# Other temporaries for the embedding's product and the stored gates, the gates' columns ahead of the sums of x, some low parts on GpSimd, and spaced gate rows and scores

## The chip, the core and the metric

The kernel runs on one core of a Trainium2 chip. The core has five engines with queues of their own: PE (TensorE: matmuls, transposes; its weight loads are listed as PEld), DVE (VectorE), ACT (ScalarE), POOL (GpSimd) and SP (SyncE, which here only issues DMAs; POOL issues some as well). An engine runs its queue in order; semaphores make it wait for others. The metric is the device time of one execution in microseconds (us), lower is better. Times of one kernel vary a little, so several runs stand beside each other, and one further execution is recorded by the hardware profiler.

## The reference

One block of a hybrid decoder on 512 positions of width 1024, all in float32, one sequence:

```
hn   = rmsnorm(x, g_mix);  proj = hn @ w_in            # 1024 x 14344
xa, ba, ca, za, q, k, v, o, zb, ig, fg, ga, gb = split(proj)
ya   = (ba * causal_short_conv(ca * xa) * silu(za)) @ w_a_out
hb   = mlstm(q, k, v, ig + b, log_sigmoid(fg + b))     # 4 heads, dk 256, dv 512
yb   = (sigmoid(o) * rmsnorm(hb) * silu(zb)) @ w_b_out
x    = x + (sigmoid(ga) * ya + sigmoid(gb) * yb) @ w_o
gate = sigmoid(rmsnorm(x, g_ple) @ w_ple_gate)
out  = rmsnorm(x + gate * (p @ w_ple), g_final)
```

In the mLSTM each head weights its scores q.k by exponentials of running sums of the gates: cumulative sums of log_sigmoid(fg), a running maximum of ig minus these sums, and the normaliser max(|den|, exp(-m)). The kernel computes it over all 512 positions at once, as a causal attention in blocks of 128.

## The kernel before

**Products.** Matmuls take float32 operands as two parts, hi and lo. ACT copies a tile into hi (`whi` for weights, line 142), DVE subtracts it from the tile to give lo (`wlo`, line 143), and PE forms hi*hi + hi*lo + lo*hi (lines 191 to 193). Weights come in operands of 512 rows and 512 columns, `wraw`, loaded by SP (line 125) into four buffers, and are split in two halves; `wlo31` is the low part of operand 3, half 1. An operand is used by 48 matmuls.

**Strassen blocks.** Where two column blocks belong together (GB; V with O of a head; ZB of two heads; GA), `strassen` makes the output of 2 x 2 blocks from seven products instead of eight. The combinations of hn, `hs`, are made once (POOL makes the sums `hsf`, `left` splits them into hi and lo). The combinations of weights are made in the raw buffers by DMAs that POOL issues with accumulation (line 146), each after the split of the half that it overwrites. Product j is done in two halves i; after each, a small generator (t1 to t6) snapshots sums with ACT (tags `s`, `v`), forms an output `c` on DVE (line 300, three buffers) and hands it to a sink.

**Order.** The order of each engine's instructions is the order in which the program emits them. After each half of a product, `step` calls `tick`: first the generators handed over at the step before, then one half of the next weight split, then one step of every generator in `active`. So one `yield` in a generator moves the rest of it one step, 12 matmuls, later. `drain` runs what is still active without anything in between.

**Around the change.** In the start stage, p @ w_ple is kept in eight temporaries `ples`, which take buffers of the tags in a string, in the order in which SP stores them (line 506). Temporaries of tags e, s and v have two buffers, of c three. Operands 1 and 2 then give the four columns of the first convolution channel block (`xa`, `ca`, `ba`, `za`), whose tasks use temporaries of tags e and c. Next PE computes the gates `psg` (line 565) from `wg`, the hi and lo parts of the gate columns of w_in in one tile, filled on DVE (lines 557, 558). A Strassen block for GB follows (operands 3 to 9), with two generators beside it: `left` (the splits of hs) and `gate_rows`, which works on `rows`, 4 partitions of 512. It ends with PE's transposes `ptc` of the rows; the queries and keys of head 0 (operands 10 and 11) come next on PE.

Per head: Q and K (a block), `scores` beside the Strassen block of V and O, the weighted sums `pv`, and after heads 0 and 2 a Strassen block for ZB of two heads. Its sink `sink_z` finishes the even head's gate and stores that of the odd head, `z_d`, which is loaded into `gt` in the odd head. In `scores`, step k of seven makes the score block `sc` k on PE and its exponentials `e` on ACT; the product `pp` (DVE), its hi copy `pr` (ACT), its lo part (DVE) and the running sum (POOL) follow.

Of the kernel before, what the change touches and what calls it, by code (L numbers as in the profile page):

```python
# [36 lines left out]
def hybrid_block(ctx, tc, x, p, g_mix, w_in, conv_w, conv_b, w_a_out, b_gates, g_head,  # L37
# [347 lines left out]
    bg = sp.tile([NH, 2], F32, name="bg")  # L385
    ss = sp.tile([P, NT], F32, name="ss")
    tmp = [sp.tile([P, NT], F32, name=f"rtmp{i}") for i in range(3)]
    ples = [temp(u, f"ple{i}") for i, u in enumerate("ssvvccee")]
    xin = sp.tile([P, NT, D], F32, name="xin", tag="xin")
    hnf = sp.tile([P, KT, S], F32, name="hnf")  # L390
    sq = hnf[:, 0:2, :].rearrange("p k s -> p (k s)")
# [120 lines left out]
    for h in range(2):  # L512
        for m in range(4):
# [5 lines left out]
            elif m % 2:  # L519
                split_half(2, m // 2)  # L520

    a11, a12 = (hnf[:, c * HC:(c + 1) * HC, :H2] for c in range(2))
    a21, a22 = (hnf[:, c * HC:(c + 1) * HC, H2:] for c in range(2))
    hsf = [sp.tile([P, HC, H2], F32, name=f"hsf{i}", tag=f"hsf{i}", align_bytes=256) for i in range(2)]
# [23 lines left out]
    for m in range(4):  # L548
# [6 lines left out]
    for g in range(2):  # L555
        src = wg_raw[:, :, g * NH:(g + 1) * NH]
        dve.tensor_copy(wg[:, :, 32 * g:32 * g + NH], src)
        dve.tensor_tensor(wg[:, :, 64 + 32 * g:64 + 32 * g + NH], src,
                          wg[:, :, 32 * g:32 * g + NH].bitcast(F32), ALU.subtract)
    for r in (0, 32):  # L560
        dve.tensor_copy(sel[r:r + NH], ident[r:r + NH, r:r + NH].unsqueeze(2).broadcast_to([NH, NH, P]))

    psg = ps_x.tile([P, S], F32, name="psg", tag="x")
    for k in range(KT):
# [13 lines left out]
    def gate_rows():  # L578
        for g, dst in enumerate((li, lf)):
            act.activation(dst, psg[64 + 32 * g:64 + 32 * g + NH, :], AF.Identity, bias=bg[:, g:g + 1])  # L580
        yield
        for g, dst in enumerate((li, lf)):
            dve.tensor_tensor(dst, dst, psg[32 * g:32 * g + NH, :], ALU.add)
        yield

        act.activation(la, lf, AF.Abs)
        act.activation(la, la, AF.Exp, scale=-1.0)
        yield
        dve.tensor_scalar(u1, la, 1.0, None, ALU.add)
        dve.scalar_tensor_tensor(off, u1, 1.0, la, ALU.subtract, ALU.subtract)  # L590
        yield
        act.activation(la, u1, AF.Ln)
        yield
        dve.scalar_tensor_tensor(lf, lf, 0.0, off, ALU.min, ALU.add)
        dve.tensor_tensor(lf, lf, la, ALU.subtract)
        yield
# [24 lines left out]
        dve.tensor_copy(nmr[0:NH], negm)  # L621
        yield
        dve.tensor_tensor(nmr[32:32 + NH], negm, nmr[0:NH].bitcast(F32), ALU.subtract)
        dve.tensor_tensor(mrow, negm, bcf, ALU.subtract)
        yield

        ptc = ps_x.tile([P, S], F32, name="ptc", tag="x")
        for n in PAIR.values():
            pe.transpose(ptc[:, 4 * n:4 * n + 4], ul[:, n, :], ident[:NH, :NH])
        for t in range(NT):  # L630
            pe.transpose(ptc[:, 40 + 4 * t:44 + 4 * t], mrow[:, t * P:(t + 1) * P], ident[:NH, :NH])
        yield
        dve.tensor_copy(colsb, ptc[:, :56])
        act.activation(enm.rearrange("p t h -> p (t h)"), colsb[:, 40:], AF.Exp)
# [39 lines left out]
            for u in range(2):  # L674
                nc.gpsimd.dma_start(yt_d[h][u], yt[u].bitcast(F32))

    def scores(h, qk, pr, pp):

        pnb = ps_x.tile([P, S], F32, name="pnb", tag="x")
        pe.matmul(pnb, lhsT=sel[:, h, :], rhs=nmr, start=True, stop=True)  # L680
# [7 lines left out]
        for k in range(NT + 3):  # L688
            if k < NT:
# [6 lines left out]
                for t in range(k, NT):  # L696
                    c = 4 * PAIR[(k, t)] + h
                    src = negd[:, t, :] if t == k else negb[:, t * P:(t + 1) * P]
                    act.activation(e[k][:, t * P:(t + 1) * P], src, AF.Exp, bias=colsb[:, c:c + 1])
            if 0 <= k - 1 < NT:  # L700
                j = k - 1
                sl = slice(POFF[j], POFF[j] + S - T0[j])
                dve.scalar_tensor_tensor(pp[:, sl], sc[j][:, T0[j]:], DK ** -0.5, e[j][:, T0[j]:], ALU.mult, ALU.mult)
                act.activation(pr[0][:, sl], pp[:, sl], AF.Copy)
            if 0 <= k - 2 < NT:
                j = k - 2
                sl = slice(POFF[j], POFF[j] + S - T0[j])
                dve.tensor_tensor(pr[1][:, sl], pp[:, sl], pr[0][:, sl].bitcast(F32), ALU.subtract)
            if 1 <= k - 3 + 0 < NT:
                j = k - 3  # L710
                sl = slice(POFF[j], POFF[j] + S - T0[j])
                pool.tensor_tensor(pp[:, T0[j]:S], pp[:, T0[j]:S], pp[:, sl], ALU.add)
            yield

    def head(h):
        qk, vv = [], []
# [25 lines left out]
                act.activation(gt[0][:, t, :], src, AF.Sigmoid)  # L742
            yield

        def begin():
            yield from scores(h, qk, pr, pp)
# [4 lines left out]
        active.append(begin())  # L751
# [34 lines left out]
        def norm(t):  # L786
            dve.scalar_tensor_tensor(y[:, t, :], y[:, t, :], hr[:, t:t + 1], gt[:, t, :], ALU.mult, ALU.mult)
# [13 lines left out]
        def sink_z(n, t, src):  # L801
            sz = temp("e", "sz")
            act.activation(sz, src, AF.Sigmoid)
            dve.tensor_tensor(sz, sz, src, ALU.mult)
            if n == 0:
                pool.tensor_tensor(gt[:, t, :], gt[:, t, :], sz, ALU.mult)
                yield
                norm(t)
            else:
                nc.gpsimd.dma_start(z_d[h + 1][:, t, :], sz)  # L810
            yield

        active.append(rsqrt())
# [253 lines left out]
```

## Time and profile before

| | us |
|---|---|
| median of 3 runs | 916.11 (913.53, 916.11, 917.68) |
| profiled execution, its time | 917.75 |
| its span, first to last instruction | 916.0 |
| PE busy in the span | 882.8 |
| DVE / ACT / POOL busy | 515.8 / 399.7 / 214.6 |
| mean granted TensorE clock | 0.987 |

In rows of the timeline the first number is the start in us from the span's beginning, the second the duration; then engine, line, operation, what is written and read, shapes and a count; in square brackets how long the engine had been idle and what ended that. In the list of waits: who waited for whom, us in total, times, the longest. A matmul's duration is modelled and overlaps the next; the distance from start to start is the better measure.

### The profile page before, as it was taken

To read this page: it belongs to the slowest core of one execution; us is meant where nothing else is said; L and a number is where in the kernel's file an instruction comes from. 1 tells how busy PE (TensorE), PEld (TensorE's weight loads), DVE (VectorE), ACT (ScalarE), POOL (GpSimd) and SP (SyncE) were. 2 spreads that over 40 slices of the span, in tenths; PEclk is the share of its full clock that TensorE was granted. 3 is DMA by queue.
4 is the path that set the end of the run, shared out by engine and by line. 5 is a ranking of instruction groups with operands and counts; after the bars stand their busy time and mean duration, and the time that the engine had idled before them with its cause. 6 is when DMAs were issued, how large, how long until landed. Compare 5 with 4: busy or idle time off the path is not lost.

```text
span 916.0 us, 10428 instructions
## 1 busy us (share of the span) xinstructions
PE 882.8 (96%) x3979; PEld 726.5 (79%) x3979; DVE 515.8 (56%) x630; ACT 399.7 (44%) x585; POOL 214.6 (23%) x205
## 2 busy tenths in 40 slices
PE   7978999998999999989999999999999999999995
PEld 6856887886888887878878888888888888888875
DVE  4578556676477566665687533234544454554446
ACT  6456456553556375553765631112222222223342
POOL 4952122232233322323144200001111112000023
PEclk9989999998999999999999999999999999999998
DMA  9778777695875688766889994665334324722002
GB/s 279 251 153 183 239 151 171 137 231 183 227 134 192 174 194 187 177 178 219 169 229 254 278 376 146 176 186 160 92 95 108 111 101 136 299 93 92 1 0 93
DMA packets 102177, 156.98 MB, mean 171 GB/s; under 512 B 5936, under 2 KB 47984, under 8 KB 100208
## 3 DMA queue, kind: packets, MB, share of 16 engines
q1 hardware_dynamic: 79984, 100.74, 34.2%
q0 software_dynamic: 22144, 55.58, 28.3%
q8 instruction: 31, 0.51, 0.2%
q14 instruction: 18, 0.15, 0.0%
HBM read 136.90 MB, written 19.40 MB: 171 GB/s over the span
## 4 chain that ended last, share of the span: by engine, by line
PE 81%; DVE 8%; ACT 4%; issue 3%; DMA 3%; POOL 1%; SPq 0%; POOLq 0%; DVEq 0%; ACTq 0%
PE mm L192 25%; PE mm L193 25%; PE mm L191 24%; DVE wlo L143 4%; ACT whi L142 2%; DMA z_d<-sz 1%; DMA wraw<-in_w_in 1%; DVE xr L973 1%; PE pv L191 1%; PE pty L670 1%; PE ptk L902 1%; PE pv L193 1%; PE pv L192 1%; DVE e L972 1%; PE sc L193 1%
## 5 line engine op out<-in xcount | busy, mean ns | idle before, releaser
L143 DVE TENSOR_TENSOR wlo<-wraw,whi 128x1024 fp32r<-128x1024 f32 x198 | 273.9, 1394 | 219.5 <-ACT whi L142 218.9
L142 ACT ACTIVATE whi<-wraw 128x1024 fp32r<-128x1024 f32 x200 | 207.9, 1053 | 160.9 <-PE mm L193 83.0
L193 PE MATMUL mm<-hn_hi,wlo 128*128 128x512 f32 x384 | 151.9, 395 | 3.1 <-DVE wlo L143 3.0
L191 PE MATMUL mm<-hn_hi,whi 128*128 128x512 f32 x384 | 152.3, 397 | 2.5 <-ACT whi L142 2.5
L192 PE MATMUL mm<-hn_lo,whi 128*128 128x512 f32 x384 | 151.1, 394 | 0.0
L146 POOL DMA_DIRECT2D wraw<-in_w_in x64 | 78.9, 1328 | 205.9 <-DVE wlo L143 189.8
L192 PE MATMUL mm<-wlo,hs 128*128 128x512 f32 x256 | 100.6, 393 | 2.7 <-DVE wlo L143 2.7
L191 PE MATMUL mm<-whi,hs 128*128 128x512 f32 x256 | 100.3, 392 | 2.7 <-DVE c L300 1.9
L193 PE MATMUL mm<-whi,hs 128*128 128x512 f32 x256 | 99.9, 390 | 0.0
L193 PEld LDWEIGHTS mm<-hn_hi,wlo 128*128 128x128 f32 x384 | 73.2, 191 | 19.6 <-DVE wlo L143 3.8
L191 PEld LDWEIGHTS mm<-hn_hi,whi 128*128 128x128 f32 x384 | 73.3, 191 | 18.1 <-ACT whi L142 3.3
L192 PEld LDWEIGHTS mm<-hn_lo,whi 128*128 128x128 f32 x384 | 73.1, 190 | 14.9
L192 PE MATMUL mm<-wlo,hn_hi 128*128 128x512 f32 x192 | 75.1, 391 | 0.2
L191 PE MATMUL mm<-whi,hn_hi 128*128 128x512 f32 x192 | 75.2, 392 | 0.0
L193 PE MATMUL mm<-whi,hn_lo 128*128 128x512 f32 x192 | 74.9, 390 | 0.0
L192 PEld LDWEIGHTS mm<-wlo,hs 128*128 128x128 f32 x256 | 48.1, 188 | 14.6 <-DVE wlo L143 5.2
L191 PEld LDWEIGHTS mm<-whi,hs 128*128 128x128 f32 x256 | 48.1, 188 | 14.1 <-ACT whi L142 1.8
L193 PEld LDWEIGHTS mm<-whi,hs 128*128 128x128 f32 x256 | 48.1, 188 | 9.9
L296 ACT ACTIVATE s<-mm 128x512 f32<-128x512 f32 x48 | 28.5, 594 | 50.6 <-PE mm L193 50.3
L191 PE MATMUL mm<-whi,yt 128*128 128x512 f32 x128 | 50.0, 391 | 0.0
L192 PE MATMUL mm<-wlo,yt 128*128 128x512 f32 x128 | 49.9, 390 | 0.0
L193 PE MATMUL mm<-whi,yt 128*128 128x512 f32 x128 | 49.9, 390 | 0.0
(245 smaller groups left out, 1336.5 us busy)
## 6 DMA issues: line engine op xcount, KB each, us to landing
wraw<-in_w_in SPq DMA_DIRECT2D x32, 1024.0 KB, 5.1
wraw<-in_w_in POOLq DMA_DIRECT2D x64, 512.0 KB, 6.1
wraw<-in_w_in SPq DMA_DIRECT2D x64, 256.0 KB, 4.2
wraw<-in_w_in SPq DMA_DIRECT2D x16, 512.0 KB, 4.9
wraw<-in_w_b_out SPq DMA_DIRECT2D x8, 1024.0 KB, 9.7
yt_d<-yc POOLq DMA_DIRECT2D x6, 1024.0 KB, 8.8
yt<-yt_d SPq DMA_DIRECT2D x6, 1024.0 KB, 6.8
wraw<-in_w_a_out SPq DMA_DIRECT2D x4, 1024.0 KB, 5.0
```

The source lines that it names most:

```text
L142: act.activation(hi, t, AF.Copy)
L143: (e_lo or dve).tensor_tensor(lo, t, hi.bitcast(F32), ALU.subtract)
L146: nc.gpsimd.dma_start(raws[to][:, ks, :], chunks[c][0][0][:, ks, :], accum_op=ALU.add)
L191: pe.matmul(ps, lhsT=a[0], rhs=b[0], start=first, stop=False, **kw)
L192: pe.matmul(ps, lhsT=a[0], rhs=b[1], start=False, stop=False, **kw)
L193: pe.matmul(ps, lhsT=a[1], rhs=b[0], start=False, stop=last, **kw)
L296: act.activation(to[i], src, AF.Copy, scale=scale)
L670: pe.transpose(pts[v][:, t * P:(t + 1) * P], y[:, t, v * P:(v + 1) * P], ident)
L902: pe.transpose(pts[k][:, t * P:(t + 1) * P], src[:, t, k * P:(k + 1) * P], ident)
L972: dve.tensor_tensor(g, g, ple[:, t, c], ALU.mult)
L973: dve.tensor_tensor(sl, sl, g, ALU.add)
```

## The change

Six edits, and none of them changes what is computed:

1. The string of tags for `ples` becomes "cccessvv": in the order of the stores, c three times, then e, s, s, v, v. Before it was "ssvvccee".
2. The filling of `wg` and `sel` is emitted ahead of the sums `hsf` of hn, after the first operand of the convolution block, not after the second.
3. In `left`, the low parts of the three combinations that have no sign change go to POOL, and each step of `left` takes two ticks.
4. `gate_rows` yields twice after each of its first six steps.
5. In `scores`, the hi copy of a product is one step later than the product, its lo part one more; POOL's sum stays. The work after the scores (the tile `gt`, and in odd heads its load from z_d) is started by a callback after step 4, not after the last.
6. In `sink_z`, the odd head's gate is multiplied in place into the sum `c` and stored from there. Before, it was stored from the sigmoid's temporary `sz` of tag e.

```
-    ples = [temp(u, f"ple{i}") for i, u in enumerate("ssvvccee")]
+    ples = [temp(u, f"ple{i}") for i, u in enumerate("cccessvv")]
...
             act.activation(hs[i][0], src, AF.Copy, scale=scale)
-            dve.scalar_tensor_tensor(hs[i][1], src, scale, hs[i][0].bitcast(F32), ALU.mult, ALU.subtract)
+            if scale == 1.0:
+                pool.tensor_tensor(hs[i][1], src, hs[i][0].bitcast(F32), ALU.subtract)
+            else:
+                dve.scalar_tensor_tensor(hs[i][1], src, scale, hs[i][0].bitcast(F32), ALU.mult, ALU.subtract)
+            yield
             yield
...
         for g, dst in enumerate((li, lf)):
             act.activation(dst, psg[64 + 32 * g:64 + 32 * g + NH, :], AF.Identity, bias=bg[:, g:g + 1])
         yield
+        yield
...
-    def scores(h, qk, pr, pp):
+    def scores(h, qk, pr, pp, done):
...
-            if 0 <= k - 1 < NT:
+            sl = {j: slice(POFF[j], POFF[j] + S - T0[j]) for j in range(k - 3, k) if 0 <= j < NT}
+            if k - 2 in sl:
+                act.activation(pr[0][:, sl[k - 2]], pp[:, sl[k - 2]], AF.Copy)
+            if k - 3 in sl:
+                dve.tensor_tensor(pr[1][:, sl[k - 3]], pp[:, sl[k - 3]], pr[0][:, sl[k - 3]].bitcast(F32), ALU.subtract)
+            if k - 1 in sl:
                 j = k - 1
-                sl = slice(POFF[j], POFF[j] + S - T0[j])
-                dve.scalar_tensor_tensor(pp[:, sl], sc[j][:, T0[j]:], DK ** -0.5, e[j][:, T0[j]:], ALU.mult, ALU.mult)
-                act.activation(pr[0][:, sl], pp[:, sl], AF.Copy)
-            if 0 <= k - 2 < NT:
-                j = k - 2
-                sl = slice(POFF[j], POFF[j] + S - T0[j])
-                dve.tensor_tensor(pr[1][:, sl], pp[:, sl], pr[0][:, sl].bitcast(F32), ALU.subtract)
-            if 1 <= k - 3 + 0 < NT:
-                j = k - 3
-                sl = slice(POFF[j], POFF[j] + S - T0[j])
-                pool.tensor_tensor(pp[:, T0[j]:S], pp[:, T0[j]:S], pp[:, sl], ALU.add)
-            yield
+                dve.scalar_tensor_tensor(pp[:, sl[j]], sc[j][:, T0[j]:], DK ** -0.5, e[j][:, T0[j]:], ALU.mult, ALU.mult)
+            if k - 3 in sl and k - 3 > 0:
+                pool.tensor_tensor(pp[:, T0[k - 3]:S], pp[:, T0[k - 3]:S], pp[:, sl[k - 3]], ALU.add)
+            yield
+            if k == NT:
+                done()
...
             act.activation(sz, src, AF.Sigmoid)
+            if n == 1:
+                dve.tensor_tensor(src, sz, src, ALU.mult)
+                nc.gpsimd.dma_start(z_d[h + 1][:, t, :], src)
+                yield
+                return
             dve.tensor_tensor(sz, sz, src, ALU.mult)
-            if n == 0:
-                pool.tensor_tensor(gt[:, t, :], gt[:, t, :], sz, ALU.mult)
-                yield
-                norm(t)
-            else:
-                nc.gpsimd.dma_start(z_d[h + 1][:, t, :], sz)
+            pool.tensor_tensor(gt[:, t, :], gt[:, t, :], sz, ALU.mult)
+            yield
+            norm(t)
             yield
```

On PE nothing changes place. On DVE, ACT and POOL it does. First DVE at the end of the start stage; before, in program order (`cu` and `cv` are the convolution's temporaries, `wlo31` the second half of operand 3):

```order
L143 TENSOR_TENSOR wlo31_485<-wraw3_339,whi31_484 128x1024
L351 TENSOR_TENSOR cu_501<-cx_482,mm_354 128x512
L352 TENSOR_SCALAR cv_502<-cu_501,prm_175 128x512
L355 SCALAR_TENSOR_TENSOR cv_502<-cu_501,prm_175,cv_502 128x510
L355 SCALAR_TENSOR_TENSOR cv_502<-cu_501,prm_175,cv_502 128x511
L359 SCALAR_TENSOR_TENSOR cv_502<-cv_502,prm_175,mm_355 128x512
L557 CAST wg_141<-wg_raw_143 128x8x4
L558 TENSOR_TENSOR wg_141<-wg_raw_143,wg_141 128x8x4
L557 CAST wg_141<-wg_raw_143 128x8x4
L558 TENSOR_TENSOR wg_141<-wg_raw_143,wg_141 128x8x4
L561 CAST sel_90<-ident_74 4x512 x2
L365 TENSOR_TENSOR cz_560<-cz_560,mm_356 128x512
```

And on DVE after the change:

```order
L143 TENSOR_TENSOR wlo20_426<-wraw2_334,whi20_425 128x1024
L143 TENSOR_TENSOR wlo21_442<-wraw2_334,whi21_441 128x1024
L524 CAST wg_141<-wg_raw_143 128x8x4
L525 TENSOR_TENSOR wg_141<-wg_raw_143,wg_141 128x8x4
L524 CAST wg_141<-wg_raw_143 128x8x4
L525 TENSOR_TENSOR wg_141<-wg_raw_143,wg_141 128x8x4
L528 CAST sel_90<-ident_74 4x512 x2
L143 TENSOR_TENSOR wlo30_472<-wraw3_339,whi30_471 128x1024
L143 TENSOR_TENSOR wlo31_491<-wraw3_339,whi31_490 128x1024
L351 TENSOR_TENSOR cu_507<-cx_488,mm_354 128x512
L352 TENSOR_SCALAR cv_508<-cu_507,prm_175 128x512
```

The five instructions on wg and sel stand ahead of operand 3's low parts and of the convolution, behind the low parts of operand 2.

Next DVE at the end of the Strassen block for GB; before (the last steps of gate_rows, with the last sums c and the splits of operands 9 and 10 between them; colsb reads PE's transposes ptc):

```order
L300 TENSOR_TENSOR c_831<-s_829,v_689 128x512
L143 TENSOR_TENSOR wlo91_834<-wraw3_339,whi91_833 128x1024
L620 TENSOR_SCALAR rows_543<-rows_543 4x512
L621 CAST nmr_88<-rows_543 4x512
L300 TENSOR_TENSOR c_857<-s_855,v_714 128x512
L143 TENSOR_TENSOR wlo100_860<-wraw7_593,whi100_859 128x1024
L623 TENSOR_TENSOR nmr_88<-rows_543,nmr_88 4x512
L624 TENSOR_TENSOR rows_543<-rows_543 4x512
L143 TENSOR_TENSOR wlo101_883<-wraw7_593,whi101_882 128x1024
L633 COPY colsb_545<-ptc_888 128x56
```

On DVE after the change, from the same last sum c on:

```order
L300 TENSOR_TENSOR c_836<-s_834,v_707 128x512
L143 TENSOR_TENSOR wlo100_839<-wraw7_593,whi100_838 128x1024
L609 SCALAR_TENSOR_TENSOR rows_543<-ones_86,rows_543 4x128 x4
L143 TENSOR_TENSOR wlo101_864<-wraw7_593,whi101_863 128x1024
L611 TENSOR_TENSOR rows_543<-rows_543 4x512
L612 COPY rows_543<-rows_543 4x128
L617 TENSOR_SCALAR rows_543<-rows_543 4x128
L618 COPY rows_543<-rows_543 4x128
L617 TENSOR_SCALAR rows_543<-rows_543 4x256
L618 COPY rows_543<-rows_543 4x128
L617 TENSOR_SCALAR rows_543<-rows_543 4x384
L618 COPY rows_543<-rows_543 4x128
```

Eleven more on the rows (lines 625 to 634 of the changed kernel) follow without anything between them, then colsb. Before, the scans (line 599) stood three products earlier, and none of what follows them stood behind wlo101.

Last POOL in the same Strassen block, before (accumulating loads into the raw buffers, the convolution's last product, stores):

```order
L146 DMA wraw3_339<-in_w_in 128x2x512 x2
L366 TENSOR_TENSOR cv_502<-cv_502,cz_560 128x512
L146 DMA wraw5_343<-in_w_in 128x2x512 x2
L544 DMA ya_d0_99<-ya0_600 128x512
L544 DMA ya_d1_100<-ya1_601 128x512
L146 DMA wraw3_339<-in_w_in 128x2x512 x2
L643 DMA sg_d0_101<-c_643 128x512
L643 DMA sg_d0_101<-c_667 128x512
L146 DMA wraw3_339<-in_w_in 128x2x512 x2
```

And on POOL after the change:

```order
L544 TENSOR_TENSOR hs01_118<-hsf0_453,hs00_117 128x1024
L146 DMA wraw5_343<-in_w_in 128x2x512
L557 DMA ya_d0_99<-ya0_596 128x512
L557 DMA ya_d1_100<-ya1_597 128x512
L146 DMA wraw3_339<-in_w_in 128x2x512
L544 TENSOR_TENSOR hs31_124<-hnf_158,hs30_123 128x1024
L146 DMA wraw3_339<-in_w_in 128x2x512
L653 DMA sg_d0_101<-c_639 128x512
L653 DMA sg_d0_101<-c_659 128x512
L146 DMA wraw3_339<-in_w_in 128x2x512
L544 TENSOR_TENSOR hs21_122<-hnf_158,hs20_121 128x1024
L146 DMA wraw3_339<-in_w_in 128x2x512
```

Each of the three low parts of hs now stands between the two halves of an accumulating load.

More of the change, by code (lines that the diff above doesn't have):

```diff
@@ L520, in hybrid_block @@
                 split_half(2, m // 2)
+    for g in range(2):
+        src = wg_raw[:, :, g * NH:(g + 1) * NH]
+        dve.tensor_copy(wg[:, :, 32 * g:32 * g + NH], src)
+        dve.tensor_tensor(wg[:, :, 64 + 32 * g:64 + 32 * g + NH], src,
+                          wg[:, :, 32 * g:32 * g + NH].bitcast(F32), ALU.subtract)
+    for r in (0, 32):
+        dve.tensor_copy(sel[r:r + NH], ident[r:r + NH, r:r + NH].unsqueeze(2).broadcast_to([NH, NH, P]))
     a11, a12 = (hnf[:, c * HC:(c + 1) * HC, :H2] for c in range(2))
@@ L552, in hybrid_block @@
         step(post(m, pss[m]))
[L555 to L561, printed above, removed]
     psg = ps_x.tile([P, S], F32, name="psg", tag="x")
@@ L591, in gate_rows @@
         yield
+        yield
         act.activation(la, u1, AF.Ln)
+        yield
         yield
@@ L595, in gate_rows @@
         dve.tensor_tensor(lf, lf, la, ALU.subtract)
+        yield
         yield
@@ L743, in sink_vo, with scored @@
             yield
-        def begin():
-            yield from scores(h, qk, pr, pp)
+        def scored():
             gt.append(hp.tile([P, NT, DV], F32, name="gt", tag="qk0", align_bytes=256))
@@ L749, in begin @@
                 nc.gpsimd.dma_start(gt[0], z_d[h])
-        active.append(begin())
+        active.append(scores(h, qk, pr, pp, scored))
         strassen(hn_lhs, sink_vo)
@@ L803, in sink_z @@
             act.activation(sz, src, AF.Sigmoid)
-            dve.tensor_tensor(sz, sz, src, ALU.mult)
-            if n == 0:
-                pool.tensor_tensor(gt[:, t, :], gt[:, t, :], sz, ALU.mult)
-                yield
-                norm(t)
-            else:
-                nc.gpsimd.dma_start(z_d[h + 1][:, t, :], sz)
+            if n == 1:
+                dve.tensor_tensor(src, sz, src, ALU.mult)
+                nc.gpsimd.dma_start(z_d[h + 1][:, t, :], src)
+                yield
+                return
+            dve.tensor_tensor(sz, sz, src, ALU.mult)
+            pool.tensor_tensor(gt[:, t, :], gt[:, t, :], sz, ALU.mult)
+            yield
+            norm(t)
             yield
```

## Prediction

> **What bounds the kernel.** I read the page's first part, then the waits of PE summed by line, then PE in order of time around each long wait, then what the engine named there was doing.
>
> ```profile
> PE 882.8 (96%) x3979; PEld 726.5 (79%) x3979; DVE 515.8 (56%) x630; ACT 399.7 (44%) x585; POOL 214.6 (23%) x205
> ...
> PE psg L565 <- DVE wg L558: 5.8, 1, 5.8
> PE mm L192 <- DVE wlo L143: 3.4, 7, 0.8
> ```
>
> PE is busy for 882.8 of 916.0 us, so 33 us of idling is all that a reordering can touch, plus slow matmuls behind the idle spells. The order of PE's own instructions is the same in both kernels; only what they wait for moves.
>
> ```profile
> 45.90 0.39 PE L193 MATMUL mm<-hn_hi,wlo 128*128 128x512 f32 x1
> 52.13 0.77 PE L565 MATMUL psg<-hn_hi,wg 128*128 128x512 f32 x1 [5.85 <-DVE wg L558]
> ...
> 55.59 0.39 PE L565 MATMUL psg<-hn_hi,wg 128*128 128x512 f32 x1
> 55.82 0.39 PE L566 MATMUL psg<-hn_lo,wg 128*128 128x512 f32 x1
> ...
> 69.30 0.47 PE L191 MATMUL mm<-whi,hs 128*128 128x512 f32 x1 [0.83 <-DVE c L300]
> 73.22 0.50 PE L191 MATMUL mm<-whi,hs 128*128 128x512 f32 x1 [0.94 <-DVE c L300]
> 77.05 0.50 PE L191 MATMUL mm<-whi,hs 128*128 128x512 f32 x1 [0.80 <-ACT v L296]
> 79.26 0.51 PE L192 MATMUL mm<-wlo,hs 128*128 128x512 f32 x1 [0.32 <-DVE wlo L143]
> ```
>
> A matmul normally starts 0.23 us after the one before (55.59 to 55.82). Behind the 5.85 us wait eight take 3.46 us (52.13 to 55.59) instead of 1.8: 1.6 us more. Behind the waits under 1 us no slow run follows.
>
> **The change, part by part**
>
> *Gates' columns, and the temporaries.*
>
> ```profile
> 31.62 6.50 DVE L143 TENSOR_TENSOR wlo<-wraw,whi 128x1024 fp32r<-128x1024 f32 x3 [0.20 <-ACT whi L142]
> 43.27 3.16 DVE L143 TENSOR_TENSOR wlo<-wraw,whi 128x1024 fp32r<-128x1024 f32 x1 [5.16 <-ACT whi L142]
> ...
> 51.79 0.19 DVE L558 TENSOR_TENSOR wg<-wg_raw,wg 128x32 fp32r<-128x32 f32 x1
> ...
> 41.69 0.60 ACT L345 ACTIVATE cx<-mm 128x512 f32<-128x512 f32 x1 [8.21 <-DMA ple_d<-ple]
> ```
>
> The four wg instructions (0.2 us each) move from behind the convolution to behind the second of the three low parts of 31.62: to about 36 us, ten ahead of PE's need at 46.3. Their price is hidden by DVE's idle 5.16 us. cx no longer shares its tag with the embedding tiles stored last, so the 8.21 us wait goes; it has no own term, but wlo and cu stop being late. Gain 5.85 + 1.6 = 7.5 us; bounds 0 and 7.5, upper end taken, since nothing else that psg reads is late. PE then reaches the Strassen products about 7 us earlier.
>
> *Gate rows spaced by empty yields.* Six extra yields push the last steps of the rows past the 14th and last step of the Strassen block; `drain` emits them in one piece, behind wlo of the next block. PE's transposes ptc come next and read them.
>
> ```profile
> 83.90:99.60 15.70, 0.00 (x0) 0.00 (x0) 6.94 (x19) 0.00 (x0) 1.00 0.91 240
> ...
> 97.09 0.60 ACT L642 ACTIVATE sg<-mm 128x512 f32<-128x512 f32 x1 [0.60 <-PE mm L193]
> 97.58 1.05 ACT L142 ACTIVATE whi<-wraw 128x1024 fp32r<-128x1024 f32 x1
> ...
> 96.35 0.69 DVE L300 TENSOR_TENSOR c<-s,v 128x512 f32<-128x512 f32 x1 [0.37 <-DMA sg_d<-c]
> ...
> 99.38 0.39 PE L193 MATMUL mm<-whi,hn_lo 128*128 128x512 f32 x1
> 99.70 0.79 PE L629 MATMUL ptc<-ident,rows 4*128 4x4 f32 x10
> ```
>
> The first row gives DVE's instructions on the rows (columns: stretch, its length, PE, PEld, DVE, ACT): 19 of them, 6.94 us, from the subtraction at 83.97 to the last one. Before, they lie between other work and end as PE does. Now all 19 stand behind wlo101, which needs whi101, which needs the sigmoid sg of the last product's first half. In before's times: whi101 ends at 98.6, wlo101 (1.2 us) at 99.9, the 19 at 106.8; PE is done at 99.8: a wait of 7.0 us. Upper end: the sum c of 96.35 already waits for the store of an earlier c; that store's sigmoid now stands behind a table load (1.28 us in each case of before), so it leaves 1.3 later, and wlo100, the scans and wlo101 follow it: 9.2 us. I take 8.6, nearer the upper end because that wait is in the trace, and 1.6 for slow matmuls after: a new loss of 10.2 us.
>
> ```profile
> 42.93 2.42 POOL L528 TENSOR_TENSOR hnf<-hsf,hnf 128x1024 f32<-128x1024 f32 x1
> ...
> 124.35 1.23 DVE L143 TENSOR_TENSOR wlo<-wraw,whi 128x1024 fp32r<-128x1024 f32 x1 [0.26 <-ACT whi L142]
> ...
> wraw<-in_w_in POOLq DMA_DIRECT2D x64, 512.0 KB, 6.1
> ```
>
> *Low parts on GpSimd.* Three of hs's four low parts (1.2 us each on DVE) become POOL instructions, 2.4 us by L528. They free DVE where the sums c are late: the waits of 0.83 and 0.94 us should go. But each stands in POOL's queue between two accumulating loads of the weights of products 4 and 6, and a low part of DVE beside a POOL instruction took 3.16 us (43.27), ended 1.1 after POOL did, where it takes 1.23 alone. Of the 2.89 us of the four waits between 69 and 80 I keep 2.0 (bounds 0 and the rival below): gain 0.9. On this the Trainium skill, "SBUF — State Buffer", section "Who interferes with whom", says that a VectorE instruction with two SBUF inputs is held for the whole of a GpSimd instruction that reads SBUF; the two rows agree. By its rule the third low part (about 72 to 74.4) would hold the last low part of product 4, PE would lose some 1.4 us there, and the sum would be about 1 us higher.
>
> *Stores of z from c instead of sz.*
>
> ```profile
> 204.96 0.62 POOL L810 DMA_DIRECT2D z_d<-sz  x1 [7.48 <-DVE sz L804]
> 207.72 0.57 POOL L810 DMA_DIRECT2D z_d<-sz  x1 [2.15 <-DVE sz L804]
> ...
> 207.37 0.69 DVE L300 TENSOR_TENSOR c<-s,v 128x512 f32<-128x512 f32 x1
> ...
> 208.18 0.62 ACT L803 ACTIVATE sz<-c 128x512 f32<-128x512 f32 x1
> 213.24 0.60 ACT L803 ACTIVATE sz<-mm 128x512 f32<-128x512 f32 x1 [4.43 <-DMA z_d<-sz]
> ...
> 214.83 0.50 PE L191 MATMUL mm<-hn_hi,whi 128*128 128x512 f32 x1 [1.39 <-ACT whi L142]
> 217.04 0.79 PE L193 MATMUL mm<-hn_hi,wlo 128*128 128x512 f32 x1 [1.47 <-DVE wlo L143]
> 221.90 0.63 PE L192 MATMUL mm<-hn_lo,whi 128*128 128x512 f32 x1
> ...
> 408.76 0.50 PE L191 MATMUL mm<-hn_hi,whi 128*128 128x512 f32 x1 [1.11 <-ACT whi L142]
> 410.97 0.80 PE L193 MATMUL mm<-hn_hi,wlo 128*128 128x512 f32 x1 [1.48 <-DVE wlo L143]
> 414.02 0.40 PE L191 MATMUL mm<-hn_hi,whi 128*128 128x512 f32 x1
> ...
> DMA to landing us min/median/max: 2.4/5.1/7.3
> ```
>
> sz has two buffers, so ACT waits for the second store, and whi and wlo of the next head's block queue behind. PE loses 1.39 + 1.47, then 11 matmuls take 4.86 us (217.04 to 221.90) where 2.5 is normal: 5.3 us. For head 2: 1.11 + 1.48 and seven in 3.05 us instead of 1.6: 4.0. Afterwards no sz is held by a store. c has three buffers, so the fourth sum of t5/t6 waits for the first store, on DVE, with wlo behind it. That store leaves at 204.96; the sz of 208.18 reuses its buffer and does not wait, so it has landed by then, and the sum of 207.37 comes 0.8 late. The low part behind it ends near 210.1; PE needs it when the block starts, six matmuls before 213.44 (214.83 less 1.39), at 212.1. The sigmoid that was late runs once the last product's first half is there, 2.7 us ahead of the block, and the second split then ends near 213, as PE gets to it. Gain 9.3, less 0.5 for what remains: 8.8 (bounds 0 and 9.3).
>
> *Scores one tick later per step.*
>
> ```profile
> 144.24 0.31 ACT L704 ACTIVATE pr<-pp 128x128 fp32r<-128x128 f32 x1 [1.49 <-DVE pp L703]
> ...
> 148.48 3.78 DVE L143 TENSOR_TENSOR wlo<-wraw,whi 128x1024 fp32r<-128x1024 f32 x2
> ...
> 151.18 0.51 PE L192 MATMUL mm<-wlo,hs 128*128 128x512 f32 x1 [0.53 <-DVE wlo L143]
> ```
>
> ACT's copy pr waited for DVE's product pp of the same tick; now it takes the one of the tick before and waits for nothing. That brings wlo of product 4 forward by about 1 us, more than the 0.53 that PE waits, in each of four heads: 4 x 0.53 = 2.1, of which I count 2.0 (bounds 0 and 2.1). The early load of z in the odd heads I cost at nothing: PE does not wait there.
>
> Sum: -7.5 + 10.2 - 0.9 - 8.8 - 2.0 = -9.0. The profiled execution took 917.75 us (span 916.0 and 1.75 around it), 1.64 over the median of 916.11, which I take off: 917.75 - 9.0 - 1.64 = 907.1, say 907.
>
> **Rivals**
>
> 1. *The sums of z wait for the stores.* Were the first store to land 7.3 us after leaving (the row's maximum), at 212.3, the sum, wlo260, two products and wlo261 (0.7 + 1.2 + 1.4 + 1.2) would end at 216.8, three too late, and slow matmuls follow: the 8.8 us shrink to 0 to 4. At the median of 5.1 us 1.3 are lost per head. Against it: the row at 208.18. About 912 to 916.
> 2. *Slower: product 4's and product 6's weights come late.* Their accumulating loads leave behind the POOL low parts. Each such load takes 6.1 us by its median, and with 2.4 of POOL, 2.3 of split and the queue the loop just fits two products (10.9 us, 48 matmuls). Were each load 6 us longer, PE would wait 6 + 1.6 twice, 15 us: 922. It decides for slower from 5.2 us per load.
> 3. *The psg wait reappears* on the low parts and banks of products 0 to 2, because DVE's convolution work has not moved as far as PE has: 5 to 7 us given back, 912 to 914. For it: DVE is slow there, beside POOL. Against: product 1 starts nine us after psg.
> 4. *ptc does not wait*, the rows' chain being done beside the last product: 907 - 10.2 = 897. Against: the order of DVE.
>
> **How the numbers follow.** Chances: forecast 0.58 (its own range 902 to 911.5: 8.6 down to 7.0, all of the four waits gone; up to half of the z or scores gain lost), rivals 0.10, 0.13, 0.08, 0.11. The range 897 to 916 takes in rivals 4, 1 and 3 and leaves out the second. 0.5% of 916.11 is 4.6 us, about what a measurement of this kernel can tell: faster is below 911.5, slower above 920.7. Faster: 0.55 + 0.04 + 0.02 + 0.11 = 0.72; same 0.17; slower 0.11.
>
> **What would show it.** PE's list of waits should lose psg on wg and gain ptc on the rows, of 7 to 9 us, with slow matmuls behind; the wait of sz for z_d should be gone, and c should wait for z_d under 1 us; PE near 151, 270, 345 and 462 should not wait for wlo. I would be wrong if ptc waits little, if POOL's three low parts end after the loads behind them are needed, or if c waits several us for z_d.

## The result, and the profile after

The changed kernel took 906.44 us (median of 906.26, 906.3, 906.58 and 908.58), the kernel before 916.89 beside it: a ratio of 0.9898, 95% interval 0.9867 to 0.9928. The profiled execution took 908.58 us, its span is 906.7 (before 916.0); it is the slowest of the four, 2.1 us above their median.

From PE's list of waits of the changed kernel (who waited for whom; us in total, times, the longest), the lines that matter:

```profile
PE mm L192 <- DVE wlo L143: 4.4, 5, 1.5
PE ptc L641 <- DVE rows L634: 4.3, 1, 4.3
PE mm L191 <- DVE c L300: 2.3, 2, 2.1
```

The wait for wg is gone and ptc waits for rows, as foreseen. Not foreseen: the waits for wlo and for the sum c became longer. PE in order of time, from psg to the first matmuls of head 0:

```profile
46.35 0.39 PE L193 MATMUL mm<-hn_hi,wlo 128*128 128x512 f32 x1
46.58 0.39 PE L569 MATMUL psg<-hn_hi,wg 128*128 128x512 f32 x1
...
63.90 0.47 PE L191 MATMUL mm<-whi,hs 128*128 128x512 f32 x1 [2.13 <-DVE c L300]
67.21 0.50 PE L192 MATMUL mm<-wlo,hs 128*128 128x512 f32 x1 [1.47 <-DVE wlo L143]
79.65 0.50 PE L192 MATMUL mm<-wlo,hs 128*128 128x512 f32 x1 [1.23 <-DVE wlo L143]
...
96.32 0.57 PE L639 MATMUL ptc<-ident,rows 4*128 4x4 f32 x3 [1.64 <-DVE rows L612]
102.47 0.58 PE L641 MATMUL ptc<-ident,rows 4*128 4x4 f32 x4 [4.26 <-DVE rows L634]
102.98 0.80 PE L191 MATMUL mm<-hn_hi,whi 128*128 128x512 f32 x1
...
106.99 0.58 PE L191 MATMUL mm<-hn_hi,whi 128*128 128x512 f32 x1
```

psg follows its neighbour after 0.23 us. The three waits in the products (2.13, 1.47, 1.23) sum to 4.83 us, where the four before had 2.89. Behind ptc nine matmuls take 4.01 us (102.98 to 106.99) instead of 2.0.

To see where time goes, each matmul's start-to-start distance beyond the normal (0.227 us after one of 512 columns, in proportion after narrower ones) was added up by stretch, for the kernel before, the changed one and all experiments. "Products" is 56 to 82 us, "rows" 82 to 110 (ptc and the matmuls behind it), "z" 200 to 230 and 400 to 430, "heads" the rest of 110 to 520 (some 5 us of it stand around narrow matmuls, 0.4 and 0.9 us a head, alike in all). The losses are those of the profiled execution. The ratio is to the kernel before, beside which each was timed; its median there was between 915.96 and 917.78, so medians of different rows compare to within 2 us only. One of the nine runs of wg_alone was slow (1102.66 us at a granted clock of 0.754) and is left out of its median.

| kernel | psg | products | rows | z | heads | median us | ratio (95%) |
|---|---|---|---|---|---|---|---|
| before | 7.7 | 4.1 | 1.2 | 12.1 | 12.8 | 916.89 | |
| changed | 0 | 6.3 | 10.6 | 2.2 | 9.4 | 906.44 | 0.9898 (0.9867-0.9928) |
| rows_tight | 0 | 6.9 | 2.7 | 2.3 | 8.1 | 900.56 | 0.9828 (0.9802-0.9855) |
| hs_on_dve | 0 | 3.7 | 11.9 | 2.2 | 8.2 | 904.97 | 0.9879 (0.9856-0.9903) |
| sel_late | 0 | 5.3 | 11.1 | 2.2 | 7.8 | 906.49 | 0.9898 (0.9874-0.9922) |
| z_from_sz | 0 | 6.2 | 10.4 | 11.0 | 8.1 | 916.64 | 0.9990 (0.9972-1.0008) |
| scores_old | 0 | 6.5 | 10.4 | 1.8 | 12.6 | 912.32 | 0.9950 (0.9932-0.9968) |
| wg_late | 7.4 | 1.3 | 11.0 | 1.8 | 8.2 | 909.64 | 0.9917 (0.9897-0.9936) |
| ples_old | 0 | 6.1 | 10.7 | 2.2 | 8.0 | 907.05 | 0.9893 (0.9873-0.9913) |
| wg_alone | 0 | 6.8 | 1.2 | 10.5 | 11.2 | 910.67 | 0.9934 (0.9912-0.9956) |
| hs_alone | 7.6 | 3.8 | 2.7 | 9.8 | 12.0 | 916.19 | 1.0005 (0.9984-1.0026) |
| tight_hs | 0 | 5.1 | 1.2 | 1.9 | 9.4 | 897.51 | 0.9796 (0.9765-0.9828) |
| tight_sel_hs | 0 | 4.3 | 1.2 | 2.0 | 8.4 | 895.38 | 0.9778 (0.9755-0.9802) |
| early | 0 | 3.3 | 1.2 | 1.9 | 8.5 | 895.36 | 0.9763 (0.9740-0.9786) |

A difference of two of these ratios is uncertain by some 0.003 (2.8 us), so parts below that are read from the traces.

**Why the products wait longer.** Busy time of the engines in the stretch of the products (stretch, its length, then PE, PEld, DVE, ACT and POOL, each with its count of instructions), of the kernel before and of the changed one:

```profile
56.00:82.00 26.00, 23.11 (x98) 17.81 (x98) 17.08 (x21) 20.19 (x25) 7.03 (x9) 1.00 0.84 179
```

```profile
56.00:82.00 26.00, 20.95 (x89) 16.06 (x88) 22.55 (x17) 19.87 (x24) 17.35 (x14) 1.00 1.01 232
```

DVE is busy for 22.55 of the 26 us with 17 instructions, before for 17.08 with 21: fewer, but longer ones. DVE and POOL of the changed kernel in that time, with the low parts of hs on POOL (L544):

```profile
57.49 3.12 DVE L199 TENSOR_TENSOR ya<-cv,ya 128x512 fp32r<-128x512 f32 x1
63.06 0.69 DVE L300 TENSOR_TENSOR c<-s,mm 128x512 f32<-128x512 f32 x1
63.67 3.49 DVE L143 TENSOR_TENSOR wlo<-wraw,whi 128x1024 fp32r<-128x1024 f32 x1
75.87 4.87 DVE L143 TENSOR_TENSOR wlo<-wraw,whi 128x1024 fp32r<-128x1024 f32 x2 [0.29 <-ACT whi L142]
91.03 0.69 DVE L300 TENSOR_TENSOR c<-s,v 128x512 f32<-128x512 f32 x1 [1.00 <-DMA sg_d<-c]
...
57.21 2.84 POOL L544 TENSOR_TENSOR hs<-hsf,hs 128x1024 fp32r<-128x1024 f32 x1
62.82 3.24 POOL L544 TENSOR_TENSOR hs<-hnf,hs 128x1024 fp32r<-128x1024 f32 x1
75.62 2.89 POOL L544 TENSOR_TENSOR hs<-hnf,hs 128x1024 fp32r<-128x1024 f32 x1
```

ya (0.68 us in a run below, alone) takes 3.12 and ends 0.6 after the POOL instruction of 57.21; the sum c three instructions later, at 63.06, is the one for which PE waits 2.13 us. The low part of 63.67 (1.2 us alone) ends at 67.16, 1.1 after POOL's, and PE's 1.47 us wait ends at 67.21. The pair of 75.87 takes 4.87 instead of 2.4, with the wait of 1.23 behind it. Each POOL low part has a wait of PE behind it; whether it makes that wait is tested below. (The row of 91.03 belongs to the wait of ptc, below.)

### The profile page after: what moved, and what is told of

Its sections match the earlier page's. It is cut to its first block, busy times and chain, and to the rows that moved or that the text cites. A ratio compares the mean times of both kernels' runs of the same rounds, so it can differ in the third digit from the quotient of the medians.

```text
span 906.7 us, 10443 instructions
## 1 busy us (share of the span) xinstructions
PE 877.6 (97%) x3979; PEld 725.1 (80%) x3979; DVE 522.1 (58%) x627; ACT 401.5 (44%) x586; POOL 220.6 (24%) x208
## 4 chain that ended last, share of the span: by engine, by line
PE 84%; DVE 6%; DMA 4%; issue 2%; POOL 2%; ACT 2%; SPq 0%; POOLq 0%; DVEq 0%; ACTq 0%
PE mm L191 26%; PE mm L193 26%; PE mm L192 26%; DMA wraw<-in_w_in 2%; DVE wlo L143 1%; PE pv L191 1%; PE pv L193 1%; PE pv L192 1%; PE pty L680 1%; PE ptk L912 1%; DVE xr L983 1%; DMA ple_d<-ple 1%; DVE e L982 1%; POOL hs L544 1%; PE sc L193 1%
```

## The experiments

All are the changed kernel with one part undone, unless said otherwise; nothing is left out of the computation in any of them.

**rows_tight: the six empty yields taken out of gate_rows.**

```
             act.activation(dst, psg[64 + 32 * g:64 + 32 * g + NH, :], AF.Identity, bias=bg[:, g:g + 1])
         yield
-        yield
```

> The changed kernel without the six empty yields in gate_rows; everything else as changed. Theory (the prediction's second term): the spacing alone makes the 19 row instructions end behind wlo101, so PE's three waits for rows (1.64, 0.16 and 4.26 us) and the slow matmuls behind them (about 1.8 us) go, and nothing else moves: 7 to 9 us less than the changed kernel's 906.4, about 898.5. Rival A: the spacing pays in the products 2 to 5, where the rows' early steps then stand ahead of late sums c again: the three waits there (4.83 us in the changed kernel) grow by 2 to 4 us and the time is 901 to 903. Rival B: the rows are late for another cause (DVE behind the low parts on GpSimd), the wait for rows stays over 3 us: 903 or more.

PE in the products and around ptc in this run:

```profile
66.93 0.50 PE L192 MATMUL mm<-wlo,hs 128*128 128x512 f32 x1 [2.71 <-DVE wlo L143]
...
86.21 0.50 PE L192 MATMUL mm<-wlo,hs 128*128 128x512 f32 x1 [0.43 <-DVE wlo L143]
92.39 0.50 PE L192 MATMUL mm<-wlo,hn_hi 128*128 128x512 f32 x1 [0.45 <-DVE wlo L143]
96.50 0.78 PE L633 MATMUL ptc<-ident,rows 4*128 4x4 f32 x10
```

ptc waits for nothing: the rows' stretch loses 2.7 us instead of 10.6. Two waits for wlo of 0.43 and 0.45 are new there. They come only where tight rows and low parts on POOL meet (hs_alone, below, has two like them; the kernel before and the kernels with tight rows and all low parts on DVE have none): the last POOL low part holds a row instruction of DVE for 2.88 us, 0.67 in tight_hs. The products lose 0.6 more, but not as rival A had it: their three waits fall from 4.83 to 3.78 us in sum (0.85 for c, 2.71 and 0.22), and some 1.6 us of slow matmuls follow the 2.71. The profiled time is 9.0 us below the changed kernel's, the median 5.9, the ratio 0.0070 (6.4 us), a little under the 7 to 9 of the theory. Spacing alone makes the wait of ptc.

**hs_on_dve: the three low parts of hs back on DVE, at the same steps.**

```
-            if scale == 1.0:
-                pool.tensor_tensor(hs[i][1], src, hs[i][0].bitcast(F32), ALU.subtract)
-            else:
-                dve.scalar_tensor_tensor(hs[i][1], src, scale, hs[i][0].bitcast(F32), ALU.mult, ALU.subtract)
+            dve.scalar_tensor_tensor(hs[i][1], src, scale, hs[i][0].bitcast(F32), ALU.mult, ALU.subtract)
```

> The changed kernel with the three low parts of hs back on DVE, at the changed kernel's places (two yields in left). Theory: the GpSimd low parts hold DVE's instructions beside them (2.8 to 3.2 us instead of 0.6 to 1.2), and so cost more than the 3.6 us of DVE time that they free: the waits of 1.47 and 1.23 us (starts near 65.8 and 78.4) go, the one of 2.13 us (near 61.8) shrinks, the time is 1 to 3 us less than the changed kernel's, about 904.5. Rival (the prediction's third term): with 1.2 us more on DVE three times, the sums c are later again and PE loses 2 us more: about 908.5.

DVE and PE of this run:

```profile
57.93 0.68 DVE L199 TENSOR_TENSOR ya<-cv,ya 128x512 fp32r<-128x512 f32 x1
62.80 1.22 DVE L143 TENSOR_TENSOR wlo<-wraw,whi 128x1024 fp32r<-128x1024 f32 x1
...
58.06 0.50 PE L192 MATMUL mm<-wlo,hn_hi 128*128 128x512 f32 x1 [1.36 <-DVE wlo L143]
63.02 0.47 PE L191 MATMUL mm<-whi,hs 128*128 128x512 f32 x1 [0.82 <-ACT hs L542]
76.36 0.50 PE L192 MATMUL mm<-wlo,hs 128*128 128x512 f32 x1 [0.58 <-DVE wlo L143]
```

ya takes 0.68 us again and the low part 1.22. The waits of 2.13, 1.47 and 1.23 are gone (0.82 for another engine and 0.58 stand in their place), one of 1.36 comes at 58.06 behind a low part of hs now on DVE. The products lose 3.7 us instead of 6.3, but the rows, which PE now reaches earlier, take 1.3 back. The median is 1.5 us lower; the ratios alone don't separate the two kernels, the waits do.

**sel_late: only sel's casts moved back to just ahead of psg.**

> The changed kernel with only the casts of sel moved back to just ahead of psg; the casts of wg stay early. Theory: the wait of 2.13 us near 61.8 comes from the lateness that DVE picks up there (sel's two casts take 5.20 us beside GpSimd's sums, 0.84 before); without them wlo30 and wlo31 end up to 4 us earlier, the convolution and the sums c follow, and the wait falls below 0.8 us: 1.3 to 2.1 us less than the changed kernel, about 904.6. Rival A: that wait comes from the first GpSimd low part (57.2), which holds the instruction of DVE ahead of the sum c: no difference, 906.4. Rival B: DVE waits only for GpSimd's sums to end, whatever stands in its queue: wlo30 and wlo31 end within 1 us of where they do now, no difference.

DVE and PE of this run:

```profile
40.33 6.78 DVE L143 TENSOR_TENSOR wlo<-wraw,whi 128x1024 fp32r<-128x1024 f32 x2
56.85 3.14 DVE L199 TENSOR_TENSOR ya<-cv,ya 128x512 fp32r<-128x512 f32 x1
...
63.27 0.57 PE L191 MATMUL mm<-whi,hs 128*128 128x512 f32 x1 [1.87 <-DVE c L300]
```

Same time, ratio 0.9898. The two low parts take 6.78 instead of 4.44 us where the casts stood, and what DVE gains by then is lost at ya, still held beside POOL's low part. My theory on sel's casts fell; rival A's figure came, and rival B fell too, since wlo31 ends 2.8 us earlier. That the low part on POOL is the only source of the c wait is not shown: wg_alone, below, has such a wait without it. Once POOL's low parts are gone, sel's place may count: tight_hs, below, with sel early loses 0.8 us more in the products than tight_sel_hs, but their times are not separated.

**z_from_sz and scores_old: the old sink_z, and the old order of scores, each alone.**

```
-            if n == 1:
-                dve.tensor_tensor(src, sz, src, ALU.mult)
-                nc.gpsimd.dma_start(z_d[h + 1][:, t, :], src)
...
+            else:
+                nc.gpsimd.dma_start(z_d[h + 1][:, t, :], sz)
```

> The changed kernel with the old sink_z: the odd head's gate is stored from sz again. Theory (the prediction's fourth term): sz waits for z_d (4.43 us), PE for whi and wlo of the next head's block, with slow matmuls behind, after heads 0 and 2: 8 to 10 us more than the changed kernel's 906.4, about 915.5. Rival: DVE and ACT stand earlier against PE in the changed kernel (scores), so the two sigmoids' waits are partly covered: 3 to 6 us more, 909.5 to 912.5.

> The changed kernel with the old order inside the step of scores (pp, pr and the low part a tick earlier each, ACT's copy in the tick of DVE's product). Theory (the prediction's fifth term): wlo of product 4 is late by 0.53 us again in each of four heads; with the short waits beside it PE loses 0.8 us a head: 2 to 3.2 us more than the changed kernel, about 909. Rival: these waits do not depend on the scores' order but on how far DVE is behind PE, which the other edits changed: within 1 us of 906.4.

ACT and PE after head 0 in z_from_sz, then ACT and DVE there in the changed kernel, then PE in scores_old:

```profile
216.22 0.60 ACT L811 ACTIVATE sz<-mm 128x512 f32<-128x512 f32 x1 [3.85 <-DMA z_d<-sz]
...
217.81 0.50 PE L191 MATMUL mm<-hn_hi,whi 128*128 128x512 f32 x1 [1.08 <-ACT whi L142]
220.03 0.80 PE L193 MATMUL mm<-hn_hi,wlo 128*128 128x512 f32 x1 [1.49 <-DVE wlo L143]
```

```profile
211.94 0.69 DVE L300 TENSOR_TENSOR c<-s,v 128x512 f32<-128x512 f32 x1 [1.00 <-DMA z_d<-c]
...
212.91 0.60 ACT L811 ACTIVATE sz<-mm 128x512 f32<-128x512 f32 x1 [0.60 <-PE mm L193]
```

```profile
155.35 0.50 PE L192 MATMUL mm<-wlo,hs 128*128 128x512 f32 x1 [0.54 <-DVE wlo L143]
```

With the store from sz the whole chain is back: sz waits for z_d, whi and wlo queue behind, z costs 11.0 instead of 2.2 us, and the ratio rises by 0.0092, 8.4 us. In the changed kernel the wait is 1.00 us, on c, and PE does not feel it. The old order of scores costs 3.2 us in the heads (ratio 0.0052 higher, 4.8 us). More than the 0.53 us waits of four heads: a matmul that waits 0.54 loses 0.8 from start to start with its neighbour, and the two odd heads, whose waits now stand at another product (279.71, and 467.15 with 468.41), lose a further 0.5 and 0.9. The two prices differ because the changed kernel's profile has a loss of its own in this stretch: 1.3 us near 500, where PE waits 0.30 and 0.75 for a split whose source landed late (ACT's copy starts at 495.14, in ples_old at 494.33). None of the kernels with one part undone has it; against ples_old's 8.0 us the old order costs 4.6. The callback after step 4 stays in scores_old, and no run undoes it: its share is not known.

**wg_late, ples_old: the filling of wg and sel, and the embedding's temporaries, as before.**

> The changed kernel with wg and sel back just ahead of psg, everything else as changed (the temporaries for the embedding's product too). Theory (the prediction's first term): PE waits for wg again, and no other part removed that wait: 5 to 7.5 us more, but DVE gains that time on PE, so the waits of products 2 to 5 (4.83 us in the changed kernel) fall to about 2 and the net is +3.5 to +5: about 910.5. Rival A: the whole 7.5 come back and the waits of products 2 to 5 stay, because they come from the GpSimd low parts alone: 914. Rival B: with cx no longer waiting for the store, the convolution ends 3 us earlier and the wait on wg is only 2 to 4 us: 907 to 909.

> The changed kernel with the old temporaries for the embedding's product. Theory: cx waits for a store of ple again and comes 3 us later (41.7 instead of 38.6), the convolution and the sums c behind it too; the wait of 2.13 us for the sum c near 61.8 grows by 1 to 3 us: 907.5 to 909.5. Rival: DVE is held by GpSimd's sums there anyway, so cu comes no later than now (49.8) and nothing changes: 906.4.

PE and DVE in wg_late:

```profile
51.39 0.77 PE L569 MATMUL psg<-hn_hi,wg 128*128 128x512 f32 x1 [5.30 <-DVE wg L561]
70.56 0.50 PE L192 MATMUL mm<-wlo,hs 128*128 128x512 f32 x1 [0.94 <-DVE wlo L143]
...
61.49 1.23 DVE L143 TENSOR_TENSOR wlo<-wraw,whi 128x1024 fp32r<-128x1024 f32 x1 [7.50 <-ACT whi L142]
```

psg costs 7.4 us again, but the products fall from 6.3 to 1.3: DVE is ahead of PE by so much that it idles 7.50 us. The net of the two stretches is 2.4 us; by the ratio it is 0.0019 (1.7 us), by the medians 3.2. So of the 7.4 us that the early wg is worth at psg, 5.0 were handed on to the products. The embedding's old temporaries change nothing (ratio 0.0005 lower, within the uncertainty), though cx waits 8.24 us for a store again: the casts of the gates' columns alone take the wait of psg away.

**wg_alone, hs_alone: the kernel before with one part added.** wg_alone has the early wg, sel and the temporaries; hs_alone the low parts on GpSimd and the second yield in left.

> The kernel before with the first part alone: other temporaries for the embedding's product, and wg and sel filled ahead of the sums of x. Theory (formed from the run with wg and sel back late, which cost only 2 to 3 us): PE, 7.5 us earlier, runs into DVE's backlog, and the products 2 to 5 take back what they took back there, about 5 us; net gain 2 to 3 us: a ratio to the kernel before of about 0.997. Rival (the prediction's first term): without the low parts on GpSimd the products 2 to 5 lose no more than before (about 4 us, as in the run with those low parts back on DVE), and the whole 7.5 us are gained: 0.992.

> The kernel before with only the three low parts of hs on GpSimd and the second yield in left. Theory: as long as PE still waits for wg and so trails DVE, the GpSimd low parts help: the loss of 4.1 us in products 2 to 5 falls to about 1.3, as in the run with wg late: 2 to 3 us less, a ratio of about 0.997. Rival: they hold DVE's instructions beside them whatever else is changed, and cost 1 to 2 us: 1.002.

PE in wg_alone:

```profile
64.58 0.47 PE L191 MATMUL mm<-whi,hs 128*128 128x512 f32 x1 [1.96 <-DVE c L300]
65.63 0.63 PE L191 MATMUL mm<-whi,hs 128*128 128x512 f32 x1
```

wg_alone gains 7.7 us at psg and gives 2.7 back in the products (4.1 to 6.8), half of what my theory said. Some 1.5 of the 2.7 are slow matmuls behind the wait of 1.96 (the row of 65.63 is one). The ratio of 0.9934 excludes the theory's 0.997 and leaves the rival's 0.992 possible. hs_alone gains nothing (1.0005): products 3.8 against 4.1, rows 2.7 against 1.2. So wg_late's 1.3 us in the products, which I had put down to GpSimd's low parts, are not theirs alone. Ahead of 110 us wg_late differs from hs_alone only in the spaced rows and the embedding's temporaries, and ples_old shows no effect of the latter: the spaced rows are worth the 2.5 us between 3.8 and 1.3, though no run had them alone. My theory for hs_alone fell too; its rival's 1.002 lies inside the interval.

**tight_hs, tight_sel_hs, early: versions to beat both.** tight_hs undoes the spacing and the low parts on GpSimd; tight_sel_hs moves sel's casts back as well; early instead casts sel near 9 us and fills wg between two splits of hn:

```
                 turn_x(HC + m)
+                if m in (1, 2):
+                    gate_columns(m - 1)
```

> The changed kernel with gate_rows without empty yields and the low parts of hs on DVE, sel's casts early as changed. Theory: of the 11 us that the three edits gained together, 3.6 more than the single edits' sum, all comes from rows and low parts (with the low parts on GpSimd the rows' instructions between them make the sums c later still), and sel's place is worth nothing here either: a ratio of 0.978. Rival: without the low parts on GpSimd, sel's casts are what makes the first sum c late, 1 to 2 us of the 11: 0.9795.

> The three edits together: gate_rows without the empty yields, the low parts of hs on DVE, sel's casts just ahead of psg. If the three theories hold and their gains add: 8.5 + 2 + 1.5 = 12 us less than the changed kernel, about 894.5. If the rivals hold for the low parts and for sel (+2 and 0): about 900.

> Rows without empty yields and low parts on DVE as in the run of the three edits, and now sel's casts near 9 us, and wg's four instructions between the splits of hn near 27 us, in gaps of DVE of 4.0 and 1.08 us. Theory: DVE's instructions from 36 to 66 us come up to 4 us earlier, so the waits of 0.78 (56.8) and 0.98 us (c, 61.6) go: 1.5 to 2 us less than the run of the three edits, a ratio of 0.976. Rival A: GpSimd's sums hold wlo30 and wlo31 to where they are now, no difference: 0.978. Rival B: wg's source lands late or its casts are held beside GpSimd's sums, the splits of hn come late and PE waits there for 1 to 3 us: 0.980.

PE in the products of tight_sel_hs:

```profile
57.82 0.50 PE L192 MATMUL mm<-wlo,hn_hi 128*128 128x512 f32 x1 [0.61 <-DVE wlo L143]
62.79 0.47 PE L191 MATMUL mm<-whi,hs 128*128 128x512 f32 x1 [0.82 <-DVE c L300]
```

tight_sel_hs takes 895.38 us, 11 less than the changed kernel: the wait of ptc is gone (rows 1.2) and the products lose 4.3. Singly the three edits gave 5.9, 1.5 and 0 by the medians, 3.6 less; that difference adds up the uncertainty of four medians and is not clear of it. In the products and rows of the profiles they gave 7.3, 1.3 and 0.5, and jointly 11.4, 2.3 more. Two losses of the single runs are missing in the joint one: the two waits for wlo that rows_tight has at 86 and 92 us (rows 2.7 against 1.2), and the 1.3 us that hs_on_dve hands on to ptc. early has no wait of 0.61 and 0.82 any more (products 3.3), but gives 0.6 back at 38 us, where wg's casts hold up wlo; the two can't be told apart by time. The ratio of tight_hs, 0.9796, lies nearest its rival's 0.9795, but the interval takes in the theory's 0.978. Both tight_sel_hs and early beat the changed kernel, by 1.2 and 1.4% (0.9778 and 0.9763 over 0.9898).

## Why the prediction was right

The forecast of 907.0 (897 to 916, faster) met 906.4. By its terms, with what the two profiles lost in the same stretch:

| term | predicted | measured |
|---|---|---|
| psg | -7.5 | -7.7 |
| new wait of ptc | +10.2 | +9.4 |
| low parts on GpSimd, products 2 to 5 | -0.9 | +2.2 |
| z stored from c | -8.8 | -9.9 |
| scores | -2.0 | -3.4 |
| sum | -9.0 | -9.4 |

DVE in the kernel before, at the start of the Strassen block:

```profile
61.93 1.23 DVE L143 TENSOR_TENSOR wlo<-wraw,whi 128x1024 fp32r<-128x1024 f32 x1 [5.11 <-ACT whi L142]
```

- *psg.* Right at its place. What failed is the step behind it, put at nothing: that PE simply reaches the products about 7 us earlier. DVE was not that far ahead: in the kernel before it idles for 5.11 us there (the row above), less than the 7.7. Alone, the part gives back 2.7 us; with it undone in the changed kernel, the products lose 5.0 less. Rival 3 had this mechanism at a chance of 0.08 and a price of 5 to 7 us; it came in part, mostly on the sum c and wlo of the products 2 to 5.
- *ptc.* Right, by its mechanism: the 19 row instructions stand behind wlo101, and ahead of that the sum c waits 1.00 us for the store of an earlier c (the row of 91.03). The wait was forecast at 8.6 us; from the end of PE's last matmul ahead of ptc (94.69) to the last four transposes (102.47) it is 7.8, in which PE makes the other ten, so the list shows 6.06 us (1.64, 0.16, 4.26) where 7 to 9 was announced. The slow matmuls behind took 2.0 instead of 1.6, and the transposes themselves were slower than before. rows_tight removes the wait by the one edit named.
- *Low parts on GpSimd.* The mis-sized term: -0.9, measured +2.2 together with what psg hands on. The step that failed is "they free DVE where the sums c are late": each holds a DVE instruction beside it by 2.3 us or more (3.12 and 3.49 instead of 0.68 and 1.2), more than the 1.2 that it frees. I had given this hold a place only at product 4, and let it do no more than lower the gain. Kernels that differ by one part in this stretch give the +2.2 in pieces: 4.1 before, 6.8 with wg early (wg_alone), 5.1 with the second yield of left as well (tight_hs), 3.7 with the rows spaced (hs_on_dve), 6.3 with the low parts on POOL (changed). So in this order POOL costs 2.6 and the spaced rows give 1.4; 1.5 of wg_alone's loss are slow matmuls that the others do not have, so that the second yield's 1.7 are mostly these. On this the prediction cited the Trainium skill, "SBUF — State Buffer", section "Who interferes with whom"; the trace agrees at all three places, and applied to all three it would have spoken against the gain.
- *z.* Right: the chain is the one described, and z_from_sz brings it back. The wait moved to c, 1.00 us against the 0.8 foreseen, and PE lost nothing of the 0.5 kept for it; that and the matmuls behind the waits, which cost 0.6 more than I had counted, make it 1.1 larger.
- *Scores.* Right in place, too small: the waits were priced at 0.53, while from start to start each costs 0.8, and odd heads lose more. Without the loss of 1.3 us near 500 the term is -4.7.

That the sum came within 0.4 us is luck: its errors of +3.1 at the products and -3.5 at the other four terms (-2.5 of it at z and scores) cancel. Rivals 1, 2 and 4 did not come.

## What to carry to other kernels

When a stall is removed, ask of every engine behind it how far it is ahead of the one that stalled: a wait that PE sits in is time in which the others catch up, and what they lack comes back as new waits (here 2.7 us alone and 5.0 among the other parts, of 7.4 to 7.7). Work moved to GpSimd is not free when VectorE works beside it: here instructions of 0.7 and 1.2 us took 3.1 and 3.5, so count what they are held against what is freed. Work spread over more steps must still end before the block does, or it is emitted in one piece where the next block waits for it.

## What the runs showed that I had not expected

Tiny casts on DVE beside POOL's sums took many times their length. In the changed kernel, DVE and POOL:

```profile
36.27 1.27 DVE L524 CAST wg<-wg_raw 128x32 fp32r<-128x32 f32 x1
37.68 2.38 DVE L524 CAST wg<-wg_raw 128x32 fp32r<-128x32 f32 x1
40.21 5.20 DVE L528 CAST sel<-ident 4x512 fp32r<-4x512 f32 x2
...
37.58 2.45 POOL L535 TENSOR_TENSOR hsf<-hnf 128x1024 f32<-128x1024 f32 x1
40.11 2.46 POOL L536 TENSOR_TENSOR hsf<-hsf,hnf 128x1024 f32<-128x1024 f32 x1
42.65 2.48 POOL L537 TENSOR_TENSOR hnf<-hsf,hnf 128x1024 f32<-128x1024 f32 x1
```

Before, these casts took 0.17 us each and 0.84 for the two of sel. Here the first of wg ends at 37.54, as POOL's earlier instructions end (37.50) and its first sum starts (37.58); the second at 40.06, as that sum ends (40.03); and sel's two last until the end of the next two sums (45.41 and 45.13): one cast per sum, although a cast has a single input. The Trainium skill, "SBUF — State Buffer", section "Who interferes with whom", says that copies and casts can enter a mode with two ports, in which VectorE and GpSimd block each other wholly; the trace agrees on the blocking, and shows nothing of the ports.

Slow matmuls do not follow from a wait's length alone. In hs_alone a like pair of waits comes after heads 0 and 2:

```profile
216.18 0.50 PE L191 MATMUL mm<-hn_hi,whi 128*128 128x512 f32 x1 [1.02 <-ACT whi L142]
218.40 0.50 PE L193 MATMUL mm<-hn_hi,wlo 128*128 128x512 f32 x1 [1.49 <-DVE wlo L143]
219.66 0.40 PE L192 MATMUL mm<-hn_lo,whi 128*128 128x512 f32 x1
...
407.90 0.50 PE L191 MATMUL mm<-hn_hi,whi 128*128 128x512 f32 x1 [1.27 <-ACT whi L142]
410.12 0.50 PE L193 MATMUL mm<-hn_hi,wlo 128*128 128x512 f32 x1 [1.49 <-DVE wlo L143]
411.32 0.63 PE L191 MATMUL mm<-hn_hi,whi 128*128 128x512 f32 x1
```

After the first none is slow (0.40 us at 219.66; the granted clock is 1.00 from 219.5 to 223), after the second eight are (0.60 to 0.63 from 410.93 on; the granted clock is 0.58 from 411 to 415), and in the changed kernel waits of 2.13 and 1.47 us at 61.8 and 65.8 leave none. The Trainium skill, "TensorE: Matmul & The Clock Gate", section "What's actually happening", says that the clock follows activity in a window of some 3.4 us that runs freely; that fits waits of like length with and without slow matmuls. By it such a loss, 1.5 to 2 us here, would come or go by where a wait falls; no run here moves a wait to test that.
